# Two-layer encoder trunk on one core: weight sums of four lead pairs made earlier and kept in DRAM, x's sums in product order, fixed rings of buffers and other store queues at the end

## The chip, the cores and the metric

One NeuronCore of a Trainium2 chip runs the whole program. The metric is device time in microseconds (us) of one execution. The engines are TensorE (PE in the profile, PEld for its weight loads), VectorE (DVE), ScalarE (ACT), GpSimd (POOL) and SyncE (SP), which here only issues DMAs. Each engine works through its own queue in order.

## The reference

```python
def _sq_relu_mlp(x, w1, w2):
    return jnp.square(jax.nn.relu(x @ w1)) @ w2

def reference(x, ...):                    # x: (1, 1024, 1024), D_FF = 4096
    for i in range(2):
        y = _short_conv_mixer(x, ...) if i == 0 else _mla_mixer(x, ...)
        x = _layer_norm(ALPHA * x + y, ln_mix_g[i], ln_mix_b[i])
        x = _layer_norm(ALPHA * x + _sq_relu_mlp(x, ff_w1[i], ff_w2[i]), ln_ff_g[i], ln_ff_b[i])
    return x
```

Layer 0 mixes tokens by a gated convolution of width 3 between two projections, layer 1 by attention over latents with 8 heads. All data are float32.

## The kernel before

A float32 matrix product is made from three float32r matmuls (`mm3`, lines 108 to 112): each operand is cut into a high part, a copy on ScalarE (line 85), and a low part, a subtraction on VectorE (line 86); high x high, high x low and low x high go into one PSUM bank.

The stages follow one another: the first mixer (lines 534 to 580; `sc_channel` makes one of eight channel blocks, `piece` loads and cuts its weights, `token_out` adds a projection to a row tile of x), the MLP of layer 0, attention, the MLP of layer 1 with the output. `ffn` (line 240) is one MLP. Each of its two matrix products is done in seven products of half size instead of eight (the Strassen-Winograd scheme), so it needs sums and differences of quarter blocks of both factors.

First matrix product: the 32 row blocks of w1 form 16 pairs p. Pair p has four quarters a11, a12, a21, a22, loaded as two "act" buffers of 512 KB (`load`, line 247). `sums` (line 252) makes on GpSimd the four combinations that products 3, 5, 6 and 7 need. `operand` cuts what product k of pair p takes. `ahead` prepares six operands in advance, in the order of the list `seq`. x stands transposed: `ln_T` transposes it on TensorE, scales it on ScalarE into `st.y` and cuts it; `combine` (line 342) makes x's four combinations, for products 5, 7, 6 and 4, column block j by column block j. Products 1 and 2 need only the first half of the tokens, product 3 only the second half. So the first four pairs, the lead (`LEAD`), run products 1 and 2 first (`begin`), while the transposes of the second half go on (`st.pump`), then product 3, and then the rest (`rest`). The results are squared after the ReLU, combined, and stored in DRAM as `hs[k, p]`.

Second matrix product: for each product k in `order2` all 16 pairs accumulate in PSUM. `second` (line 381) loads a piece of h and a quarter of w2 (line 390), subtracts for the combination (line 394 for k = 4 on GpSimd, line 398 on VectorE) and cuts both. k = 4 is last: it runs over token tiles (0, 1), then 2, then 3, and loads its left operands by `left` (line 377). `done` adds a product to the output rows (line 441), and `finish` normalizes a row tile: `keep_z` in layer 0, `emit` (line 903) in layer 1, which scales, adds and stores the output. The first four row tiles are finished while k = 7 runs (`post`), the last four in the passes of k = 4.

Buffers are taken from pools: "act" (34 of 128x1024), "fp" (8, cut operands), "half" (19 of 128x512). A buffer is given out again when the last use of its tile is over. A planner in the framework orders each engine's queue and hands out the buffers ahead of time; the program text gives only priorities and dependencies.

Of the kernel before, what the change touches and what calls it, by code (L numbers as in the profile page):

```python
# [12 lines left out]
P = 128  # L13
# [25 lines left out]
def trunk_kernel(ctx, tc, x, xT, w_sci, w_sco, w_lat, w_qk, w_rv, w_o, w_f1, w_f2, gvec, grow, rope, out):  # L39
# [111 lines left out]

    def ln_stats(xr):
        s = stat(24)
# [12 lines left out]

    def ln_z(xr):
        mu, r, _ = ln_stats(xr)
        nc.vector.tensor_scalar(xr, xr, mu, r, op0=ALU.subtract, op1=ALU.mult)
# [52 lines left out]
    def last_chunk(l, lhs_of, wps, xrs, first, zs):  # L222
        st = Stage(True)
        for t in range(NT):
# [15 lines left out]
    def ffn(l, lnl, st, zs, xa, hs, out_l, finish, early=None):  # L240

# [5 lines left out]
        def load(p):  # L247
            raw[p] = [act1(F32), act1(F32)]
            for i in range(2):
                nc.sync.dma_start(raw[p][i], w_f1[l, p + NPAIR * i])  # L250

        def sums(p):
            (a11, a12), (a21, a22) = [(r[:, 0:HB], r[:, HB:T]) for r in raw[p]]
            s1 = s1w[p] = hbt()
            nc.gpsimd.tensor_tensor(s1, a21, a22, op=ALU.add)  # L255
            nc.gpsimd.tensor_tensor(a21, a11, a21, op=ALU.subtract)  # L256
            nc.gpsimd.tensor_tensor(a11, s1, a11, op=ALU.subtract)  # L257
            nc.gpsimd.tensor_tensor(a12, a12, a11, op=ALU.subtract)

        def operand(p, k):  # L260
            r1, r2 = raw[p]
            src = {1: r1[:, 0:HB], 2: r1[:, HB:T], 3: r1[:, HB:T], 4: r2[:, HB:T], 5: s1w.get(p),
                   6: r1[:, 0:HB], 7: r2[:, 0:HB]}[k]
            wh, wl = fpair()
            split(src, wh, wl)
            return wh, wl
# [6 lines left out]
        def ahead(n):  # L273
            while seq and len(ready) < n:
                p, k = seq.pop(0)
                if p not in raw:
                    load(p)
                if k == (3 if p < LEAD else 6):
                    sums(p)
                ready[p, k] = operand(p, k)  # L280
            if not seq and len(ready) < 4:
                ahead2(4 - len(ready))

        def product(p, k):
            ahead(AHEAD)
            wp = ready.pop((p, k))
            ps = psB()
# [14 lines left out]
        def rest(p):  # L302
# [36 lines left out]
            for k, a in ((1, a11), (4, a22), (5, s1), (6, s2), (7, s3), (2, a12), (3, s4)):  # L339
                nc.sync.dma_start(hs[k, p], a)  # L340

        def combine(j):
            b11, b12 = st.y[j][:, 0:HB], st.y[j][:, HB:T]
            b21, b22 = st.y[j + 4][:, 0:HB], st.y[j + 4][:, HB:T]
# [23 lines left out]
        def part(d, p):  # L368
            if p // 2 not in d:
                d[p // 2] = act1(F32)  # L370
            return d[p // 2][:, (p % 2) * HB:(p % 2 + 1) * HB]

        def left(k, p, js):
# [7 lines left out]
        def second(k, p):  # L381
# [62 lines left out]
        for k in order2[:-1]:  # L444
# [20 lines left out]
        passes = ((0, 1), (2,), (3,))  # L465
        todo = [(js, p) for js in passes for p in range(NPAIR)]
        lefts, wps = {}, {}
        for js in passes:
            pss = [psB() for _ in js]
            for p in range(NPAIR):  # L470
# [10 lines left out]
                if p % 4 == 1:  # L481
                    st2.pump(1)
                if early and js == passes[-1] and p in (10, 12, 14):
                    early()
            for j, ps in zip(js, pss):
                done(4, j, ps)
                finish(4 + j, xrs)
        if out_l is not None:
# [63 lines left out]
    for half in range(2):  # L552
# [4 lines left out]
        yt[0, half], carry = gate(0, half, *pss, carry)  # L557
    xrs = [xrt() for _ in range(NT)]
    for t in range(NT):
        nc.vector.tensor_copy(xrs[t][:, 0:1], carry[:, 0:1])  # L560
        nc.gpsimd.dma_start(xrs[t], x[t * P:(t + 1) * P])
# [12 lines left out]
    wso = [piece(w_sco[i]) for i in range(4)]  # L574
# [11 lines left out]

    def keep_z(t, xrs):
        ln_z(xrs[t])
        nc.gpsimd.dma_start(spill[t * P:(t + 1) * P], xrs[t])
# [10 lines left out]

    st, xrs = ffn(0, 0, st, zs[0], xa, hs, 1, keep_z, early_lat)
    stage.__exit__(None, None, None)
# [299 lines left out]

    def emit(t, xrs):
        if not ogr:
            ogr.extend(ln_rows(3, hbt))
        gr = ogr
        xr = xrs[t]
        mu, r, s = ln_stats(xr)
# [12 lines left out]
    ffn(1, 2, st, zs[1], xa, hs, None, emit)  # L921
    stage.__exit__(None, None, None)
# [59 lines left out]
```

## Time and profile before

| what | value |
|---|---|
| median of 3 runs | 2119.86 us (2118.95 to 2119.93) |
| profiled execution | 2118.39 us, its span 2116.6 us |
| granted TensorE clock, mean | 0.989 of full speed |
| instructions | 27650 |
| bytes moved by DMA | 299.93 MB, mean 142 GB/s |

The span runs from the first to the last instruction; the rest of the execution's own time lies around it. Busy time of an engine is the sum of its instructions' time. The view by stretches gives each engine's busy time and number of instructions (x) in a stretch, the granted clock (1.00 is 2.4 GHz, 0.50 is 1.2 GHz) and the DMA share. In a timeline, a row's last bracket says how long the engine stood idle before the instruction and whose end it waited for.

### The profile page before, as it was taken

How to read it: one execution, taken by the hardware profiler on the slowest of the kernel's cores; microseconds unless marked ns; L12 is line 12 of the kernel's file. 1: busy time of each engine (PE TensorE's matmuls, PEld its weight loads, DVE VectorE, ACT ScalarE, POOL GpSimd, SP SyncE). 2: the span in 40 equal slices, each digit the busy share in tenths (PEclk: the TensorE clock that was granted, in tenths of full speed). 3: DMA queues.
4: the chain of work that ended last, by engine and by line, in shares of the span. 5: the costliest groups of instructions: out<-in, count | busy, mean ns of one | idle time of the engine just before them, and what ended most of it. 6: DMA issues, size and time to landing. Idle time of an engine off the chain costs nothing. (4 is left out here: it accounts for less than half of the span.)

```text
span 2116.6 us, 27650 instructions
## 1 busy us (share of the span) xinstructions
PE 2051.6 (97%) x9592; PEld 1702.5 (80%) x9592; DVE 1509.2 (71%) x2586; ACT 939.9 (44%) x1775; POOL 444.9 (21%) x399
## 2 busy tenths in 40 slices
PE   8999999799999999999999999999799999999987
PEld 6888888688888788888888888778688887888865
DVE  5333438887785697878467778878986785796877
ACT  4110213554454553345556665324644464543343
POOL 1000001535651000130000002313355630000252
PEclk9999999899999999999999999999899999999998
DMA  5310213066553986643100001213256545995522
GB/s 171 120 49 31 70 53 141 31 225 212 196 197 121 362 309 200 204 131 120 50 7 22 16 27 58 88 70 130 93 197 225 207 152 195 335 339 160 183 96 77
DMA packets 151820, 299.93 MB, mean 142 GB/s; under 512 B 17008, under 2 KB 32368, under 8 KB 151680
## 3 DMA queue, kind: packets, MB, share of 16 engines
q1 hardware_dynamic: 140976, 265.88, 36.7%
q0 software_dynamic: 7392, 26.26, 3.4%
q10 hardware_dynamic: 3312, 6.03, 0.9%
q8 instruction: 75, 1.23, 0.2%
q14 instruction: 65, 0.53, 0.1%
HBM read 214.21 MB, written 83.89 MB: 141 GB/s over the span
## 5 line engine op out<-in xcount | busy, mean ns | idle before, releaser
L110 PE MATMUL pB<-act,fp 128*128 128x512 f32 x1024 | 403.4, 395 | 21.6 <-ACT act L85 14.5
L111 PE MATMUL pB<-act,fp 128*128 128x512 f32 x1024 | 402.2, 393 | 6.2 <-DVE act L86 6.2
L112 PE MATMUL pB<-act,fp 128*128 128x512 f32 x1024 | 403.2, 394 | 4.7 <-DVE fp L86 4.4
L86 DVE TENSOR_TENSOR fp<-act,fp 128x512 fp32r<-128x512 f32 x352 | 307.0, 877 | 129.1 <-ACT fp L85 128.6
L85 ACT CAST fp<-act 128x512 fp32r<-128x512 f32 x352 | 213.7, 617 | 309.3 <-PE pB L112 151.2
L111 PE MATMUL pB<-fp,act 128*128 128x512 f32 x768 | 299.4, 390 | 3.2 <-DVE fp L86 2.9
L110 PE MATMUL pB<-fp,act 128*128 128x512 f32 x768 | 297.8, 390 | 4.0 <-ACT fp L85 2.5
L112 PE MATMUL pB<-fp,act 128*128 128x512 f32 x768 | 298.6, 389 | 0.0
L110 PEld LDWEIGHTS pB<-act,fp 128*128 128x128 f32 x1024 | 193.7, 189 | 66.8 <-ACT act L85 17.4
L112 PEld LDWEIGHTS pB<-act,fp 128*128 128x128 f32 x1024 | 193.9, 189 | 51.0 <-DVE fp L86 11.2
L111 PEld LDWEIGHTS pB<-act,fp 128*128 128x128 f32 x1024 | 194.2, 190 | 47.7 <-DVE act L86 7.9
L110 PE MATMUL pB<-act,w 128*128 128x512 f32 x536 | 210.1, 393 | 6.7 <-ACT w L85 6.1
L111 PE MATMUL pB<-act,w 128*128 128x512 f32 x536 | 209.9, 392 | 0.3 <-DVE act L86 0.2
L112 PE MATMUL pB<-act,w 128*128 128x512 f32 x536 | 209.3, 391 | 0.0
L293 DVE TENSOR_TENSOR half<-half,pB 128x512 f32<-128x512 f32 x232 | 155.0, 681 | 59.7 <-PE pB L112 56.8
L110 PEld LDWEIGHTS pB<-fp,act 128*128 128x128 f32 x768 | 144.0, 188 | 35.3 <-ACT fp L85 3.4
L111 PEld LDWEIGHTS pB<-fp,act 128*128 128x128 f32 x768 | 144.2, 188 | 34.9 <-DVE fp L86 5.3
L112 PEld LDWEIGHTS pB<-fp,act 128*128 128x128 f32 x768 | 144.1, 188 | 30.0
L110 PE MATMUL pB<-w,act 128*128 128x512 f32 (+1 forms) x480 | 164.9, 344 | 1.6 <-DVE act L142 0.7
L111 PE MATMUL pB<-w,act 128*128 128x512 f32 (+1 forms) x480 | 163.4, 341 | 1.3 <-DVE w L86 1.3
L112 PE MATMUL pB<-w,act 128*128 128x512 f32 (+1 forms) x480 | 162.6, 340 | 0.0
L86 DVE TENSOR_TENSOR act<-half,act 128x512 fp32r<-128x512 f32 x198 | 147.6, 749 | 16.5 <-ACT act L85 16.3
(154 smaller groups left out, 3312.1 us busy)
## 6 DMA issues: line engine op xcount, KB each, us to landing
h<-half SPq DMA_DIRECT2D x224, 256.0 KB, 2.4
half<-h SPq DMA_DIRECT2D x192, 256.0 KB, 4.7
half<-in_w_f SPq DMA_DIRECT2D x160, 256.0 KB, 4.3
act<-in_w_f SPq DMA_DIRECT2D x64, 512.0 KB, 4.6
act<-in_w_f SPq DMA_DIRECT2D x64, 256.0 KB, 4.3
raw<-in_w_sci SPq DMA_DIRECT2D x42, 256.0 KB, 2.7
z<-act POOLq DMA_DIRECT2D x16, 512.0 KB, 3.1
act<-z SPq DMA_DIRECT2D x16, 512.0 KB, 3.9
```

The source lines that it names most:

```text
L85: nc.scalar.copy(hi, src)
L86: nc.vector.tensor_tensor(lo, src, hi.bitcast(F32), op=ALU.subtract)
L110: nc.tensor.matmul(ps, lh, rh, start=first, stop=False)
L111: nc.tensor.matmul(ps, lh, rl, start=False, stop=False)
L112: nc.tensor.matmul(ps, ll, rh, start=False, stop=last)
L293: nc.vector.tensor_tensor(o, a, b, op=op)
```

## The change

- The weight sums of the four lead pairs of both layers are made during channels 1 to 3 of the first mixer (`lead_sums`): two loads on GpSimd's queue, four GpSimd operations, three stores to DRAM tiles `ws`. A small copy from the last channel's result holds each load back to its channel. x's row tiles are loaded after that, one channel before their first use.
- In the MLP, a lead pair loads only its first row for products 1 and 2. `fetch` loads the sums of products 3 and 6 with one DMA before product 3, and those of 7 and 5, with the plain quarter of product 4, before product 6. All of them go through SyncE's queue.
- x's sums become a list of `chores`: two of the subtractions first, then the cuts for product 6, those for 7, then differences and cuts for 5 and 4. All sums of x are VectorE's. The second half's transposes come in the order 4, 0, 5, 1, 6, 2, 7, 3, four after each of the first two `begin`s.
- In k = 4, the left operands use a ring of six "half" buffers and the w2 quarters a ring of three.
- The statistics of the half of a row tile that k = 4 does not change are taken in the middle of its pass.
- The output stores leave SyncE for GpSimd's queue, except those of the last tile. Tiles 4 to 6 multiply and add on VectorE.

```diff
+    def ln_half(xr, s, d):
         st = s[:, 0:12].rearrange("p (a b) -> p a b", a=2)
-        for d in range(2):
+        nc.vector.bn_stats(st[:, d], xr[:, d * HB:(d + 1) * HB])
...
-        st.add_T(l, 1, xrs, (4, 5, 6, 7, 0, 1, 2, 3))
+        st.add_T(l, 1, xrs, (4, 0, 5, 1, 6, 2, 7, 3))
...
+    def weight_sums(r, s1):
+        (a11, a12), (a21, a22) = [(a[:, 0:HB], a[:, HB:T]) for a in r]
+        nc.gpsimd.tensor_tensor(s1, a21, a22, op=ALU.add)
+        nc.gpsimd.tensor_tensor(a21, a11, a21, op=ALU.subtract)
+        nc.gpsimd.tensor_tensor(a11, s1, a11, op=ALU.subtract)
+        nc.gpsimd.tensor_tensor(a12, a12, a11, op=ALU.subtract)
+
+    def lead_sums(l, p, ws, after):
+        r = [act1(F32), act1(F32)]
+        s1 = act1(F32)[:, 0:HB]
+        for i in range(2):
+            nc.vector.tensor_copy(r[i][:, 0:1], after)
+            nc.gpsimd.dma_start(r[i], w_f1[l, p + NPAIR * i])
+        weight_sums(r, s1)
+        nc.gpsimd.dma_start(ws[:, 0:T], r[0])
+        nc.gpsimd.dma_start(ws[:, T:T + HB], r[1][:, 0:HB])
+        nc.gpsimd.dma_start(ws[:, T + HB:2 * T], s1)
...
-            raw[p] = [act1(F32), act1(F32)]
-            for i in range(2):
-                nc.sync.dma_start(raw[p][i], w_f1[l, p + NPAIR * i])
+            raw[p] = [act1(F32) for _ in range(1 if p < LEAD else 2)]
+            for i, r in enumerate(raw[p]):
+                nc.sync.dma_start(r, w_f1[l, p + NPAIR * i])
...
+        def fetch(p, k):
+            if k == 3:
+                raw[p] = [act1(F32), None]
+                nc.sync.dma_start(raw[p][0], ws[p][:, 0:T])
+            else:
+                raw[p][1] = act1(F32)
+                nc.sync.dma_start(raw[p][1][:, 0:HB], ws[p][:, T:T + HB])
+                nc.sync.dma_start(raw[p][1][:, HB:T], w_f1[l, p + NPAIR, :, HB:T])
+                s1w[p] = hbt()
+                nc.sync.dma_start(s1w[p], ws[p][:, T + HB:2 * T])
...
-                if k == (3 if p < LEAD else 6):
+                if p < LEAD and k in (3, 6):
+                    fetch(p, k)
+                elif k == 6:
                     sums(p)
...
+        def chore(k):
+            while len(xc.get(k, ())) < 4:
+                chores.pop(0)()
+
         def product(p, k):
             ahead(AHEAD)
+            chore(k)
...
         def combine(j):
-            for k, o, a, b in ((5, b11, b12, b11), (7, b12, b22, b12), (6, b22, b22, b11), (4, b21, b22, b21)):
-                (nc.gpsimd if k == 7 else nc.vector).tensor_tensor(o, a, b, op=ALU.subtract)
-                h, lo = act()
-                split(o, h, lo)
-                xc.setdefault(k, []).append((h, lo))
+            add(block(12, j), block(22, j), block(12, j), ALU.subtract)
+            add(block(11, j), block(12, j), block(11, j))
+
+        def diff(k, b, j):
+            a = (22, 11) if k == 5 else (11, 21)
+            add(block(b, j), block(a[0], j), block(a[1], j), ALU.subtract)
+            cut(k, b, j)
+
+        chores += [lambda j=j: combine(j) for j in range(4)]
+        chores += [lambda j=j: cut(6, 11, j) for j in range(4)] + [lambda j=j: cut(7, 12, j) for j in range(4)]
+        chores += [lambda j=j: diff(5, 22, j) for j in range(4)] + [lambda j=j: diff(4, 21, j) for j in range(4)]
...
-        for p in range(LEAD):
+        for p, n in enumerate((4, 4, 0, 0)):
             begin(p)
-            st.pump(2)
+            st.pump(n)
+            if p:
+                for _ in range(2 if p < 3 else 4):
+                    chores.pop(0)()
...
             add(held[p][2], held[p][0], product(p, 3))
-            combine(p)
+            for _ in range(2):
+                chores.pop(0)()
...
+            if not lring:
+                lring.extend(hbt() for _ in range(6))
...
-            hr = hbt()[:, 0:n]
+            hr = lring[nleft[0] % len(lring)][:, 0:n]
+            nleft[0] += 1
...
-            w = part(ta, p) if k == 1 else part(tb, p) if k == 3 else hbt()
+            if k == 4 and not wring:
+                wring.extend(hbt() for _ in range(3))
+            w = part(ta, p) if k == 1 else part(tb, p) if k == 3 else wring[p % 3] if k == 4 else hbt()
...
+                if p == 9:
+                    for j in js:
+                        half_stats(j)
...
-    for c in range(1, 5):
-        sc_channel(c)
+    for c in range(1, 4):
+        for l, p in early_sums[3 * c - 3:3 * c]:
+            lead_sums(l, p, wss[l][p], carry[:, 0:1])
+        carry = sc_channel(c)
+    xrs = [xrt() for _ in range(NT)]
+    for t in range(NT):
+        nc.vector.tensor_copy(xrs[t][:, 0:1], carry[:, 0:1])
+        nc.gpsimd.dma_start(xrs[t], x[t * P:(t + 1) * P])
+    sc_channel(4)
...
-            if t == NT - 1 or (t == NT - 2 and d == 0):
+            if t == NT - 1:
...
-                (nc.gpsimd if d else nc.vector).tensor_tensor(xr[:, c], xr[:, c], gr[d], op=ALU.mult)
-                nc.gpsimd.tensor_tensor(xr[:, c], xr[:, c], gr[2 + d], op=ALU.add)
-            (nc.scalar if t == NT - 1 and d == 0 else nc.sync).dma_start(out[t * P:(t + 1) * P, c], xr[:, c])
+                last = t >= NT // 2
+                (nc.gpsimd if d and not last else nc.vector).tensor_tensor(xr[:, c], xr[:, c], gr[d], op=ALU.mult)
+                (nc.vector if last else nc.gpsimd).tensor_tensor(xr[:, c], xr[:, c], gr[2 + d], op=ALU.add)
+            (nc.sync if t == NT - 1 and d else nc.scalar if t == NT - 1 else nc.gpsimd).dma_start(
+                out[t * P:(t + 1) * P, c], xr[:, c])
```

## Rows read from the trace of the kernel before

**Rows 1.** The page, share of busy time: us, share, instructions.

```profile
PE 2051.6 (97%) x9592; PEld 1702.5 (80%) x9592; DVE 1509.2 (71%) x2586; ACT 939.9 (44%) x1775; POOL 444.9 (21%) x399
```

**Rows 2.** View by stretches: stretch, length, busy us (x instructions), clock, DMA share, GB/s.

```profile
47.00:176.00 129.00, 129.00 (x571) 106.85 (x570) 50.23 (x94) 25.32 (x45) 4.22 (x8) 1.00 0.25 87
176.00:361.00 185.00, 185.00 (x834) 153.73 (x833) 86.71 (x162) 33.18 (x59) 3.20 (x6) 1.00 0.22 74
390.00:421.00 31.00, 20.14 (x73) 14.56 (x71) 28.43 (x40) 17.78 (x32) 9.65 (x7) 0.78 0.05 17
1485.00:1515.00 30.00, 18.85 (x67) 13.72 (x66) 27.43 (x39) 16.48 (x30) 9.39 (x7) 0.77 0.05 18
2005.00:2048.00 43.00, 40.09 (x175) 32.17 (x174) 43.00 (x65) 20.82 (x39) 29.01 (x18) 1.00 0.33 108
2048.00:2084.00 36.00, 29.04 (x107) 21.04 (x106) 15.73 (x38) 9.15 (x25) 5.09 (x4) 0.86 0.24 72
2084.00:2107.60 23.60, 22.89 (x98) 17.71 (x96) 22.09 (x56) 10.74 (x33) 11.05 (x8) 1.00 0.25 87
2107.60:2116.60 9.00, 0.26 (x2) 0.00 (x0) 5.15 (x12) 0.29 (x1) 0.12 (x1) 0.65 0.23 87
```

**Rows 3.** Timeline of the first lead: start, length, engine, line, operation, idle before.

```profile
362.86 0.50 PE L110 MATMUL pB<-act,fp 128*128 128x512 f32 x1 [0.71 <-ACT fp L85]
...
372.82 33.59 SPq L340 DMA_DIRECT2D h<-half  x4
...
381.17 1.04 PE L174 MATMUL pB<-ident,act 128*128 128x128 f32 x8
...
382.10 0.62 ACT L85 CAST fp<-act 128x512 fp32r<-128x512 f32 x1 [3.34 <-POOL act L258]
...
389.48 3.48 DVE L346 TENSOR_TENSOR act<-act 128x512 f32<-128x512 f32 x2
...
401.90 0.68 DVE L86 TENSOR_TENSOR fp<-half,fp 128x512 fp32r<-128x512 f32 x1
402.50 0.68 DVE L346 TENSOR_TENSOR act<-act 128x512 f32<-128x512 f32 x1
...
413.62 1.22 PE L110 MATMUL pB<-act,fp 128*128 128x512 f32 x2 [6.15 <-ACT act L85]
```

**Rows 4.** Groups of GpSimd's instructions: count, busy us, mean ns, idle before.

```profile
L255 POOL TENSOR_TENSOR half<-act 128x512 f32<-128x512 f32 x32 | 44.8, 1401 | 36.1 <-ACT half L329 36.1
...
L918 POOL TENSOR_TENSOR act<-act,half 128x512 f32<-128x512 f32 x13 | 20.7, 1610 | 1.5 <-DVE act L917 1.2
...
L227 POOL DMA_DIRECT2D z<-act x16 | 8.6, 536 | 373.1 <-DVE act L169 333.8 <-DVE stat L163 25.4 <-PE pB L112 13.9
```

**Rows 5.** Timeline of the second layer's tail.

```profile
2040.31 1.74 POOL L394 TENSOR_TENSOR act<-act,half 128x512 f32<-128x512 f32 x1
...
2048.38 0.34 SPq L390 DMA_DIRECT2D half<-in_w_f  x1
...
2050.45 0.39 PE L110 MATMUL pB<-act,fp 128*128 128x512 f32 x1
...
2051.50 1.29 POOL L394 TENSOR_TENSOR act<-act,half 128x512 f32<-128x512 f32 x1 [9.46 <-DMA half<-in_w_f]
...
2052.83 0.62 ACT L85 CAST act<-act 128x512 fp32r<-128x512 f32 x1 [8.99 <-POOL act L394]
```

**Rows 6.** Waits of SyncE's queue, 2030 to 2066: total us, times, longest.

```profile
SPq L919 <- POOL act L918: 8.5, 4, 3.4
SPq L390 <- DVE fp L86: 6.2, 1, 6.2
```

**Rows 7.** The page, DMA issues: count, KB each, median us to landing.

```profile
act<-in_w_f SPq DMA_DIRECT2D x64, 512.0 KB, 4.6
```

**Rows 8.** Timeline of the end, the ScalarE queue's store.

```profile
2112.63 0.35 ACTq L919 DMA_DIRECT2D out<-act  x1
```

More of the change, by code (lines that the diff above doesn't have):

```diff
@@ L150, in newton, with ln_stats @@
         nc.vector.tensor_tensor(r, r, t, op=ALU.mult)
-    def ln_stats(xr):
-        s = stat(24)
+    def ln_half(xr, s, d):
         st = s[:, 0:12].rearrange("p (a b) -> p a b", a=2)
-        for d in range(2):
+        nc.vector.bn_stats(st[:, d], xr[:, d * HB:(d + 1) * HB])
+    def ln_stats(xr, s=None):
+        cols = (0, 1) if s is None else (0,)
+        s = stat(24) if s is None else s
+        st = s[:, 0:12].rearrange("p (a b) -> p a b", a=2)
+        for d in cols:
             nc.vector.bn_stats(st[:, d], xr[:, d * HB:(d + 1) * HB])
@@ L165, in ln_stats, with ln_z @@
         return mv[:, 0:1], r, s
-    def ln_z(xr):
-        mu, r, _ = ln_stats(xr)
+    def ln_z(xr, s=None):
+        mu, r, _ = ln_stats(xr, s)
         nc.vector.tensor_scalar(xr, xr, mu, r, op0=ALU.subtract, op1=ALU.mult)
@@ L236, in trunk_kernel, with ffn @@
     LEAD = 4
+    def weight_sums(r, s1):
[14 more added lines that the diff above has]
+        nc.gpsimd.dma_start(ws[:, T + HB:2 * T], s1)
     AHEAD = 6
     AHEAD2 = 4
-    def ffn(l, lnl, st, zs, xa, hs, out_l, finish, early=None):
+    def ffn(l, lnl, st, zs, xa, hs, ws, out_l, finish, early=None):
         xc = {1: st.xt[0][0:4], 2: st.xt[0][4:8]}
@@ L247, in load @@
         def load(p):
-            raw[p] = [act1(F32), act1(F32)]
-            for i in range(2):
-                nc.sync.dma_start(raw[p][i], w_f1[l, p + NPAIR * i])
+            raw[p] = [act1(F32) for _ in range(1 if p < LEAD else 2)]
+            for i, r in enumerate(raw[p]):
+                nc.sync.dma_start(r, w_f1[l, p + NPAIR * i])
         def sums(p):
[L253 to L258, printed above, removed]
+            s1w[p] = hbt()
+            weight_sums(raw[p], s1w[p])
+        def fetch(p, k):
[6 more added lines that the diff above has]
+                nc.sync.dma_start(raw[p][1][:, HB:T], w_f1[l, p + NPAIR, :, HB:T])
+                s1w[p] = hbt()
+                nc.sync.dma_start(s1w[p], ws[p][:, T + HB:2 * T])
         def operand(p, k):
-            r1, r2 = raw[p]
-            src = {1: r1[:, 0:HB], 2: r1[:, HB:T], 3: r1[:, HB:T], 4: r2[:, HB:T], 5: s1w.get(p),
-                   6: r1[:, 0:HB], 7: r2[:, 0:HB]}[k]
+            src = s1w[p] if k == 5 else raw[p][k in (4, 7)]
+            if k != 5:
+                src = src[:, 0:HB] if k in (1, 6, 7) else src[:, HB:T]
             wh, wl = fpair()
@@ L340, in rest, with block, cut @@
                 nc.sync.dma_start(hs[k, p], a)
+        def block(k, j):
+            return {11: st.y[j][:, 0:HB], 12: st.y[j][:, HB:T],
+                    21: st.y[j + 4][:, 0:HB], 22: st.y[j + 4][:, HB:T]}[k]
         def combine(j):
-            b11, b12 = st.y[j][:, 0:HB], st.y[j][:, HB:T]
-            b21, b22 = st.y[j + 4][:, 0:HB], st.y[j + 4][:, HB:T]
-            for k, o, a, b in ((5, b11, b12, b11), (7, b12, b22, b12), (6, b22, b22, b11), (4, b21, b22, b21)):
-                (nc.gpsimd if k == 7 else nc.vector).tensor_tensor(o, a, b, op=ALU.subtract)
-                h, lo = act()
-                split(o, h, lo)
-                xc.setdefault(k, []).append((h, lo))
+            add(block(12, j), block(22, j), block(12, j), ALU.subtract)
+            add(block(11, j), block(12, j), block(11, j))
+        def cut(k, b, j):
+            h, lo = act()
+            split(block(b, j), h, lo)
+            xc.setdefault(k, []).append((h, lo))
+        def diff(k, b, j):
[5 more added lines that the diff above has]
+        chores += [lambda j=j: diff(5, 22, j) for j in range(4)] + [lambda j=j: diff(4, 21, j) for j in range(4)]
         for p in range(LEAD):
             load(p)
-        for p in range(LEAD):
+        for p, n in enumerate((4, 4, 0, 0)):
             begin(p)
-            st.pump(2)
+            st.pump(n)
+            if p:
+                for _ in range(2 if p < 3 else 4):
+                    chores.pop(0)()
         st.pump(len(st.todo))
@@ L465, in ffn, with half_stats @@
         passes = ((0, 1), (2,), (3,))
+        early_s = {}
+        def half_stats(j):
+            early_s[j] = stat(24)
+            ln_half(xrs[4 + j], early_s[j], 1)
         todo = [(js, p) for js in passes for p in range(NPAIR)]
@@ L486, in ffn @@
                 done(4, j, ps)
-                finish(4 + j, xrs)
+                finish(4 + j, xrs, early_s[j])
         if out_l is not None:
@@ L557, in trunk_kernel @@
         yt[0, half], carry = gate(0, half, *pss, carry)
[L558 to L561, printed above, removed]
     def sc_channel(c):
@@ L570, in sc_channel @@
             yt[c, half], carry = gate(c, half, *pss, carry)
-    for c in range(1, 5):
-        sc_channel(c)
+        return carry
+    wss = [[dr.tile([P, 2 * T], F32, name="ws%d_%d" % (l, p)) for p in range(LEAD)] for l in range(DEPTH)]
+    early_sums = [(l, p) for l in range(DEPTH) for p in range(LEAD)]
+    for c in range(1, 4):
[7 more added lines that the diff above has]
+    sc_channel(4)
     wso = [piece(w_sco[i]) for i in range(4)]
@@ L585, in trunk_kernel, with keep_z @@
     spill = dr.tile([T, D], F32, name="spill")
-    def keep_z(t, xrs):
-        ln_z(xrs[t])
+    def keep_z(t, xrs, s=None):
+        ln_z(xrs[t], s)
         nc.gpsimd.dma_start(spill[t * P:(t + 1) * P], xrs[t])
@@ L901, in trunk_kernel, with emit @@
     ogr = []
-    def emit(t, xrs):
+    def emit(t, xrs, s=None):
         if not ogr:
@@ L907, in emit @@
         xr = xrs[t]
-        mu, r, s = ln_stats(xr)
+        mu, r, s = ln_stats(xr, s)
         nc.vector.tensor_scalar(s[:, 17:18], mu, r, -1.0, op0=ALU.mult, op1=ALU.mult)
```

6 lines of the change are left out of this document (4 added, 2 removed).

## The prediction

> **What bounds the kernel now.** I read the share of busy time first: TensorE is busy 97% of the span [rows 1], so the time is TensorE's work plus its holes, and this change takes no matmul away. Only a hole that is filled can shorten it, so I looked for holes next, with the view that cuts the span into stretches [rows 2]. The full pace is in the row 176 to 361: 834 matmuls in 185.00 us, 0.222 us each. Held against that pace, four stretches of [rows 2] are short of matmuls:
>
> - first lead, 390 to 421: 73 matmuls are worth 16.2 us, the stretch has 31.0, so 14.8 are lost;
> - second lead, 1485 to 1515: 67 are worth 14.9 of 30.0, 15.1 lost;
> - tail, 2005 to 2107.6: 38.8 of 43.0, 23.7 of 36.0 and 21.7 of 23.6, so 4.2, 12.3 and 1.9 lost, 18.4 together;
> - the end, 9.0 us in which TensorE has nothing left.
>
> The granted clock is part of this: it is 1.00 at full pace (2.4 GHz) and 0.78, 0.77 and 0.86 in the three worst stretches, that is, some of their matmuls ran at 1.2 GHz, after TensorE had stood still. A count held against the full pace holds the waits and the clock together, so neither is added again. Outside these four, the start apart, the holes are small, and the change does not touch them.
>
> The timeline says why the leads are short [rows 3]. GpSimd makes the four weight sums of four lead pairs just when VectorE wants to make x's sums. ScalarE stood 3.34 us before a weight cast, until a GpSimd sum (L258) came, and VectorE's subtractions queue behind such casts. When VectorE gets to x's sums, two of them take 3.48 us beside GpSimd (389.48), 1.74 each, against 0.68 when GpSimd is still (402.50). Then combine runs j by j over all four products, so the four pieces of the first product needed (k = 6) come last to first hand: TensorE waits 6.15 us in one place (413.62), for a cast of x.
>
> In the tail the timeline shows another chain [rows 5, 6]. SyncE's queue is in order. It stands at output stores (L919) until GpSimd's additions are through, 8.5 us in four waits, then 6.2 us at a load of w2 (2048.38), whose "half" buffer had last served a piece of h whose split on VectorE was late. The GpSimd subtraction behind that load starts after 9.46 us of idleness (2051.50), ScalarE's cast of it at 2052.83, and behind that cast, in the same queue, stands the cast of a left operand that TensorE waits for. The same goes on at the next three pairs; most of the 12.3 us lies in these four gaps.
>
> **The change part by part.** *Lead sums made early.* Per layer it takes 16 GpSimd operations out of the lead and puts 32 in all into the first mixer, at 1.40 us each by the row of L255 [rows 4]: 45 us of GpSimd between 47 and 176, where GpSimd is busy 4.22 of 129 us [rows 2]. If each slows one VectorE instruction from 0.68 to 1.74 us [rows 3], VectorE gets 32 x 1.06 = 34 us on top of 50.23, 84 of 129 us. TensorE runs that stretch at full pace (571 in 129.00), so the cover is 45 us of VectorE idleness; without it, at most those 34 us would be paid. Lower bound 0, upper bound 34; I take 0. The Trainium skill ("SBUF — State Buffer", Who interferes with whom) says that a VectorE instruction with two SBUF inputs and a GpSimd instruction that reads SBUF exclude one another, the later one waiting out the other. The 1.74 beside 0.68 us [rows 3] agrees, and the rule speaks against the new place of the sums as much as for emptying the old one; by it, too, the first mixer pays 34 us of VectorE time, which idleness covers.
>
> The loads and stores of the sums ride on GpSimd's own queue, 5 DMAs a pair, 40 in all at 0.54 us of issue (L227, [rows 4]), 22 us. Sums and issue make 67 of 129 us. x's eight loads now stand behind them on that queue and start a channel (144 x 0.222 = 32 us) before their first use; a load of 512 KB lands in 4.6 us [rows 7]. I cost that at nothing; if the queue is late by more than that channel, the residual additions wait, and I give that up to 10 us in the range only.
>
> *The lead after it.* The fetches are SyncE's: per pair one half-megabyte load instead of two, then one of 512 KB and three of 256 KB. SyncE stood 33.59 us at four stores here [rows 3], so it has the room, if the fetches come ahead of those stores. No GpSimd arithmetic is left in the lead, so VectorE's price is 0.60 us from start to start (401.90 to 402.50, [rows 3]). Up to the product k = 4 of pair 0 it has 21 weight cuts, 4 cuts of x^T, 16 x sums, 16 cuts of these and 13 additions of products, 70 instructions, 42 us, and some 3 us of the last LayerNorm (estimate): from 362 to 407. TensorE, from 362.86, needs 15 products x 12 x 0.222 = 40.0 us and four double groups of transposes at 0.8 us net (1.04 us shown for one, [rows 3]), 3.2 us: it wants the last product at 406 and the last x piece at 408. So the order by product just fits, and VectorE is the tight engine. A queue never runs without gaps; I leave 3 us of loss in each lead. Lower bound 0, upper 8: the "act" buffers. By my count, x^T (12), y (8) and the three finished products' x pieces (12) hold 32 of 34 when k = 4 wants its first, and weights of pairs 2 and 3 want the other two; a wait like the 6.15 us at 413.62 can come back there. Gain 14.8 - 3 + 15.1 - 3 = 23.9 us.
>
> *Rings and stores.* The w2 loads of k = 4 get three buffers of their own, the left pieces six. Load p then waits for subtraction p - 3 and no longer for a VectorE split. Stores on GpSimd's queue no longer stop SyncE. They come behind the additions they wait for on the same engine, so they block nothing new but GpSimd itself: eight stores x 0.54 = 4.3 us in the stretch 2005 to 2048, where it is busy 29.01 of 43 [rows 2]. The last subtractions then start near 2040.31 + 4.3 = 2045 [rows 5]; five of them, two with a load of about 2.5 us ahead, are through by 2053, and TensorE, whose k = 4 begins at 2050.45 [rows 5] and takes six matmuls, 1.33 us, a pair, wants the first of these five at 2050.5 + 11 x 1.33 = 2065. The wait goes; of the 12.3 us I leave 2. VectorE is busy 43.00 of 43.00 us just before [rows 2] and is not relieved, so the 4.2 stay, and the 1.9 stay: tiles 4 to 6 give VectorE ten more operations, 6.0 us at 0.60, less two longer ones of today, and take GpSimd's, 1.61 us each [rows 4], from beside its splits. Gain 10.3; bounds 0 (the same wait at another buffer) and 15.
>
> The Trainium skill ("SBUF — State Buffer", Summary: rules for kernel authors) advises against a GpSimd-queue DMA under VectorE work, because descriptor writing is starved while VectorE is in a two-port mode; its section A bandwidth-pool intuition that's wrong gives about 3.1 us for one so overlapped. The stores of z took 0.54 us on GpSimd beside a working VectorE [rows 4], so the trace does not show it here; by the page, eight stores would be 25 us instead of 4.3.
>
> *The rest.* The statistics of one half ahead of time: TensorE does not wait for them, and in the chain after the last matmul one such instruction stands now too; 0. After the last matmul the chain to the ScalarE store at 2112.63 and its landing [rows 8] is the same: 9.0 us stay. Rings in the first layer: no hole there, 0.
>
> **Sum.** 23.9 + 10.3 = 34.2 us off the profiled execution's 2118.39 gives 2084.2; the median of the runs is 1.5 above it, so 2085.7, forecast 2086.
>
> **The rivals.** *The tail keeps its wait*: GpSimd's queue is late (eight stores at several times 0.54 us, or subtractions ordered behind all of them), or a late left split stops SyncE before the w2 load as it does now. For it: VectorE at 43.00 of 43.00; against: ring buffers free long before. Then 23.9 only: 2096. *The act buffers bind in the leads*: each keeps 8 us: 2096. For it: my count of 34; against: each finished x sum frees two buffers. *Both*: 2106. *Fetches late*, the other side: a fetch gets its act buffer only when an earlier pair's last cut frees one, or stands in SyncE's queue behind a store that waits for ScalarE, as L340 does for 33.59 us [rows 3]. Each that TensorE sees costs 4.6 us of load [rows 7] and 1.3 of cast and subtraction, 5.9 us; there are eight groups a layer, 16. Six of them eat the 34.2; ten give 2145. Against it: these loads depend on nothing but a buffer, and can go out while the last LayerNorm runs. *The change does not do what it says*: VectorE, with the same 32 x operations, is the bound of the lead anyway and the rest goes on as it is: only some 3 us a lead and the tail's, 2104. Against it: its 28.43 busy us in 390 to 421 [rows 2] come after idling earlier, behind GpSimd.
>
> **Chances.** Forecast 0.53 (its own range 2079 to 2093: 1 to 5 us left in each lead, 7 to 13 gained in the tail), tail keeps its wait 0.15, act buffers 0.12, both 0.05, no relief 0.05, late fetches 0.07, cancelling within 0.2% (4 us, about what a measurement tells from no change) 0.03. Range 2075 (nothing left in the leads, 15 gained in the tail) to 2106: it holds the forecast and all rivals but late fetches. Faster 0.90, same 0.03, slower 0.07.
>
> **What would show it.** Right: in both leads some 135 to 140 matmuls per 31 us and clock 1.00, no GpSimd sums there, x sums at 0.6 us; no SyncE wait at a w2 load of k = 4 over 2 us, no 9 us GpSimd gap; the first mixer still at 0.222 us a matmul. Wrong: a TensorE wait for a cast of x at k = 5 or 4 of pair 0; waits of SyncE's fetches for a buffer; left splits late behind VectorE in the last passes, or GpSimd sums still running when x's loads should go out.

## The result, and the profile after

The changed kernel takes 2083.36 us in the median (2080.19 to 2086.86) against 2119.89: ratio 0.9831, 95% interval 0.9818 to 0.9843, or 35.8 us less (33.3 to 38.6). The forecast was 2086, its range 2075 to 2106. The profiled execution is the longest of the four, 2086.86 us with a span of 2085.1. Line numbers are those of the changed kernel: L456 is the GpSimd subtraction for k = 4 (L394 before), L437 and L452 SyncE's loads of h and w2 (L377, L390), L332 VectorE's additions (L346, L293), L994 to L996 the multiplication, addition and store of the last LayerNorm (L917 to L919). Cuts are still L85 and L86.

The page's row of busy shares answers to [rows 1]: TensorE's instructions are the same 9592.

```profile
PE 2044.7 (98%) x9592; PEld 1706.3 (82%) x9592; DVE 1505.8 (72%) x2618; ACT 938.8 (45%) x1776; POOL 453.0 (22%) x437
```

The view by stretches, with the columns of [rows 2]. The first mixer and the stretch after it come first, then the two leads, then the tail cut in the same lengths as there, counted back from the end of the span:

```profile
47.00:176.00 129.00, 129.00 (x571) 106.92 (x570) 71.65 (x109) 25.13 (x45) 67.28 (x80) 1.00 0.66 218
176.00:361.00 185.00, 185.00 (x835) 153.79 (x834) 86.76 (x162) 33.61 (x60) 3.20 (x6) 1.00 0.20 66
390.00:421.00 31.00, 31.00 (x139) 25.67 (x138) 28.33 (x47) 19.05 (x35) 0.28 (x1) 1.00 0.60 201
1470.00:1500.00 30.00, 30.00 (x134) 24.88 (x133) 27.98 (x47) 19.20 (x35) 0.00 (x0) 1.00 0.60 198
1973.50:2016.50 43.00, 40.76 (x173) 33.24 (x173) 43.00 (x63) 21.32 (x41) 39.65 (x28) 0.96 0.34 109
2016.50:2052.50 36.00, 31.19 (x128) 25.29 (x127) 20.41 (x45) 10.56 (x28) 9.24 (x5) 0.91 0.24 73
2052.50:2076.10 23.60, 22.92 (x100) 18.04 (x98) 18.90 (x62) 11.01 (x34) 3.24 (x6) 1.00 0.37 118
2076.10:2085.10 9.00, 0.36 (x2) 0.00 (x0) 5.15 (x12) 0.29 (x1) 0.00 (x0) 0.81 0.19 73
```

At 0.222 us a matmul the leads lose nothing: 139 matmuls are worth 30.9 of 31.0 us, 134 are worth 29.7 of 30.0, at the full clock (2.4 GHz). The whole 14.8 + 15.1 us is back. The tail's three stretches held 380 matmuls before and hold 401 now, worth 89.0 of 102.6 us: 13.6 us are still lost where 18.2 were (the prediction's 18.4, with its rounding). So the tail gave 4.6 us. The end is 9.0 us as before.

The timeline of the first lead answers to [rows 3]. VectorE makes x's sums early and at 0.6 us each. SyncE's fetches of product 3's sums (L282) are out by 378.0, and the fetches before product 6 (L285) begin right behind them; their last ones go out between 393 and 399:

```profile
372.09 0.69 DVE L332 TENSOR_TENSOR act<-act 128x512 f32<-128x512 f32 x1 [1.36 <-ACT act L180]
...
375.16 1.89 DVE L332 TENSOR_TENSOR act<-act 128x512 f32<-128x512 f32 x3
...
376.69 1.29 SPq L282 DMA_DIRECT2D act<-ws  x3
...
378.08 0.38 SPq L285 DMA_DIRECT2D act<-ws  x1
...
382.50 1.89 DVE L332 TENSOR_TENSOR act<-act 128x512 f32<-128x512 f32 x3
```

TensorE's list of waits from 361 to 421 has one row left, where [rows 3] had a single wait of 6.15 us:

```profile
PE pB L110 <- ACT fp L85: 0.7, 1, 0.7
```

GpSimd's groups answer to [rows 4]: one of the four sums, as it runs in the first mixer, and the stores of the last LayerNorm from 1960 to 2052.

```profile
L246 POOL TENSOR_TENSOR act<-act 128x512 f32<-128x512 f32 x8 | 10.4, 1297 | 0.3
...
L996 POOL DMA_DIRECT2D out<-act x8 | 4.5, 564 | 0.3 <-POOL act L995 0.3
```

The tail's timeline answers to [rows 5, 6]. It has a new chain:

```profile
2009.64 1.52 ACT L992 ACTIVATE act<-act,stat 128x512 f32<-128x512 f32 x2 [6.80 <-DVE stat L985]
...
2011.25 10.94 POOL L994 TENSOR_TENSOR act<-act,half 128x512 f32<-128x512 f32 x1 [2.16 <-ACT act L992]
2011.33 0.68 DVE L994 TENSOR_TENSOR act<-act,half 128x512 f32<-128x512 f32 x1
2011.93 1.28 DVE L86 TENSOR_TENSOR act<-act 128x512 fp32r<-128x512 f32 x2
...
2019.15 1.88 DVE L86 TENSOR_TENSOR act<-act 128x512 fp32r<-128x512 f32 x3
2022.15 2.52 POOL L995 TENSOR_TENSOR act<-act,half 128x512 f32<-128x512 f32 x2
2024.62 1.11 POOL L996 DMA_DIRECT2D out<-act  x2
2027.92 0.62 ACT L85 CAST act<-act 128x512 fp32r<-128x512 f32 x1 [9.48 <-DMA out<-act]
2028.45 1.93 ACT L85 CAST fp<-half 128x256 fp32r<-128x256 f32 x6
...
2028.90 0.80 PE L110 MATMUL pB<-act,fp 128*128 128x512 f32 x1 [4.81 <-ACT fp L85]
```

Read it from the bottom. TensorE waits 4.81 us for a left operand's cast. That cast stands on ScalarE behind the cast of a w2 piece, which has waited 9.48 us for an "act" buffer. The buffer is that of output tile 3, whose store came at 2024.62, after two additions, after a multiplication (L994) that took 10.94 us where its kind takes 1.3 to 1.75. It started while VectorE was in one subtraction, and VectorE went on with sixteen more instructions that have both inputs in SBUF, without a pause; the last ended at 2021.03.

The wait that the rings were to take away is gone. The last L456 ends at 1991.87, when the first tile's L994 begins; before, five came after 2040. In SyncE's waits from 1973.5 to 2076.1 none at the load of w2 is over 1.3 us ([rows 6] had 6.2 in one); its long ones are at loads into the left ring, and none of TensorE's waits leads back to them:

```profile
SPq L437 <- DVE fp L86: 69.7, 26, 41.9
SPq L452 <- POOL act L456: 8.9, 9, 1.3
```

Of the page's DMA issues [rows 7], the early loads on GpSimd's queue land a little later; the last row is the store that answers to [rows 8], 3.87 us before the end of the span (3.97 before):

```profile
act<-in_w_f POOLq DMA_DIRECT2D x16, 512.0 KB, 5.1
```

```profile
2081.23 0.35 ACTq L996 DMA_DIRECT2D out<-act  x1
```

### The profile page after: what moved, and what is told of

The parts are those of the page before. It is cut to its first block, busy times and chain, and to the rows that moved or that the text cites. A ratio compares the mean times of both kernels' runs of the same rounds, so it can differ in the third digit from the quotient of the medians.

```text
span 2085.1 us, 27812 instructions
## 1 busy us (share of the span) xinstructions
PE 2044.7 (98%) x9592; PEld 1706.3 (82%) x9592; DVE 1505.8 (72%) x2618; ACT 938.8 (45%) x1776; POOL 453.0 (22%) x437
## 4 chain that ended last, share of the span: by engine, by line
PE 84%; DVE 6%; DMA 3%; POOL 2%; ACT 2%; issue 2%; SPq 0%; DVEq 0%; ACTq 0%; POOLq 0%
PE pB L112 26%; PE pB L111 26%; PE pB L110 26%; DVE act L86 1%; PE pB L881 1%; DVE fp L86 1%; PE pB L179 1%; DMA raw<-in_w_o 1%; DMA half<-in_w_f 1%; DMA act<-in_xT 1%; ACT tmp L752 1%; PE pA L849 1%; POOL act L994 1%; PE pA L850 1%; PE pA L851 1%
## 5 line engine op out<-in xcount | busy, mean ns | idle before, releaser
L86 DVE TENSOR_TENSOR fp<-act,fp 128x512 fp32r<-128x512 f32 x352 | 294.8, 843 | 117.3 <-ACT fp L85 116.8
L85 ACT CAST fp<-act 128x512 fp32r<-128x512 f32 x352 | 212.9, 617 | 274.9 <-PE pB L112 139.2
L332 DVE TENSOR_TENSOR half<-half,pB 128x512 f32<-128x512 f32 x232 | 155.2, 681 | 67.2 <-PE pB L112 64.3
L86 DVE TENSOR_TENSOR act<-half,act 128x512 fp32r<-128x512 f32 x198 | 151.2, 769 | 15.4 <-ACT act L85 15.4
```

The costliest lines, as they stand in the source:

```text
L85: nc.scalar.copy(hi, src)
L86: nc.vector.tensor_tensor(lo, src, hi.bitcast(F32), op=ALU.subtract)
L332: nc.vector.tensor_tensor(o, a, b, op=op)
```

## Experiments

"Gain" is (1 - ratio) x 2119.9 us, with the ratio's interval. "Tail lost" is 102.6 us less 0.222 us for each matmul in the three tail stretches of the run's profile, cut as above. The changed kernel: gain 35.8, tail lost 13.6; the kernel before: 0 and 18.2.

| run | median us | ratio (95%) | gain us | tail lost us |
|---|---|---|---|---|
| lead_only | 2088.45 | 0.9865 (0.9850 to 0.9879) | 28.6 | 19.1 |
| tail_only | 2114.21 | 0.9985 (0.9975 to 0.9995) | 3.2 | 8.7 |
| dram_only | 2097.00 | 0.9905 (0.9891 to 0.9920) | 20.1 | |
| order_only | 2114.78 | 0.9985 (0.9976 to 0.9994) | 3.2 | |
| dve_emit | 2074.13 | 0.9782 (0.9768 to 0.9797) | 46.2 | 2.9 |
| rings_only | 2084.29 | 0.9834 (0.9815 to 0.9853) | 35.2 | 11.1 |
| no_rings | 2091.75 | 0.9867 (0.9851 to 0.9884) | 28.2 | 18.5 |
| sp_stores | 2082.68 | 0.9821 (0.9805 to 0.9837) | 37.9 | 11.8 |
| tile3_dve | 2077.25 | 0.9800 (0.9787 to 0.9814) | 42.4 | 5.6 |
| dve_norings | 2080.57 | 0.9818 (0.9804 to 0.9831) | 38.6 | 10.2 |
| dve_nohalf | 2071.93 | 0.9775 (0.9762 to 0.9788) | 47.7 | 0.9 |
| dve_sp | 2075.28 | 0.9795 (0.9782 to 0.9808) | 43.5 | 3.4 |

### The lead and the tail apart

lead_only takes the tail's edits back; tail_only keeps only them, on the kernel before.

```diff
 # lead_only, against the changed kernel
-            hr = lring[nleft[0] % len(lring)][:, 0:n]
+            hr = hbt()[:, 0:n]
-            w = ... else wring[p % 3] if k == 4 else hbt()
+            w = ... else hbt()
-                if p == 9:
-                    for j in js:
-                        half_stats(j)
 # and the last LayerNorm with its stores as before
```

> The changed kernel's lead (sums of four pairs kept in DRAM, x's sums by product) with the tail of the kernel before. Theory, from the trace after the change: the leads run at full pace, so all of their loss goes, 14.8 + 15.1 = 30 us: about 2090, and the tail's stretch loses its 18 us as before. Rival, the prediction as written: the leads keep 3 us each and the tail gave 10: about 2096.

> The lead of the kernel before with the rings, early half statistics, new last LayerNorm and GpSimd stores. Theory: the tail's gain is only about 5 us (13.5 lost after against 18.4 before): about 2115. Rival, the prediction as written: 10.3 us, about 2109.5.

lead_only gained 28.6 us (25.7 to 31.8). That holds the 30 that the traces give and not the 23.9 of the prediction; its 2088.45 is near the theory's 2090. tail_only gained 3.2 (1.1 to 5.3): less than the 10.3 of the prediction. The two make 31.8, the whole change 35.8; the intervals leave that difference open. tail_only's own profile leaves it open too: it shows 8.7 us lost in the tail, a gain of 9.5, in an execution of 2111.44 us; that is one of the shortest of its nine, which go up to 2116.86. The multiplication that takes 10.94 us in the changed kernel takes 1.31 there (see "The held multiplication").

### The lead's two parts

dram_only has the sums in DRAM and x's sums in the old order, with one of the four x sums (k = 7) on GpSimd again and the second half's transposes in their old order. order_only has the four pairs' weight sums on GpSimd in the lead, and x's sums by product, all on VectorE. Both have the old tail. "The order" below means these edits together: product order, the k = 7 sums moved to VectorE, the transposes' order. No run takes them apart.

```diff
 # dram_only, against lead_only
-            chore(k)
-        for p, n in enumerate((4, 4, 0, 0)):
+        for p in range(LEAD):
             begin(p)
-            st.pump(n)
+            st.pump(2)
-            for _ in range(2):
-                chores.pop(0)()
+            combine(p)
```

> Weight sums kept in DRAM, but x's sums in the old order (tile by tile over all four products, k = 7 on GpSimd), old tail. Theory: both parts are needed. GpSimd's 16 sums are gone from the lead, but the first product still gets its pieces last, and the 6 us wait of each lead stays: 30 - 12 = 18 us gained, about 2102. Rival A, contention with GpSimd is all: about 2090, no wait for x's casts. Rival B, the order is all: under 5 us gained, 2115 or more.

> x's sums by product and all on VectorE, but the four pairs' weight sums made in the lead by GpSimd as before; old tail. Theory: both parts are needed. The weight sums still hold up weight casts and double the price of VectorE's sums: about 12 us gained, 2108, with VectorE's subtractions at some 1.7 us beside GpSimd. Rival A, contention is all: 2115 or more. Rival B, the order is all: about 2090.

dram_only came out at 20.1 (17.0 to 23.1), as the theory had it. order_only gained 3.2 (1.3 to 5.1), not 12: here the rival "contention is all" comes closer. Counted from 361 to 421, the first lead holds 213 matmuls before, 223 with the order alone, 260 with the DRAM sums alone and 278 with both. VectorE's groups from 375 to 421 in order_only say why the order is worth little by itself:

```profile
L300 DVE TENSOR_TENSOR act<-act 128x512 f32<-128x512 f32 x15 | 20.5, 1407 | 0.0
```

Fifteen x sums at 1407 ns, beside GpSimd sums of 1620. VectorE is full for the whole stretch, so another order alone can't bring the pieces in time:

```profile
390.00:421.00 31.00, 23.38 (x90) 17.52 (x89) 31.00 (x45) 17.74 (x33) 5.80 (x4) 0.94 0.07 26
```

In the changed kernel, from 361 to 421, the same instruction costs half:

```profile
L332 DVE TENSOR_TENSOR act<-act 128x512 f32<-128x512 f32 x16 | 10.4, 686 | 1.4 <-ACT act L180 1.4
```

With GpSimd's weight sums out of the way the order is worth the rest: 28.6 - 20.1 = 8.5 us, with about 3 us of uncertainty on either figure. The wait that it takes away is smaller in dram_only than the 6 us of before, so the theory had the gain right and the wait too long. In the second lead TensorE stands at

```profile
1488.00 1.22 PE L110 MATMUL pB<-act,fp 128*128 128x512 f32 x2 [2.46 <-ACT act L85]
```

The two parts do not seem additive, 20.1 + 3.2 against 28.6; the difference is about what the intervals allow. The first lead's counts go the same way: 47 and 10 matmuls more by one part alone, 65 by both. That fits an order that pays once VectorE has the time for it.

### The held multiplication

dve_emit takes GpSimd's arithmetic out of the last LayerNorm; sp_stores leaves it there and changes only the queue of the stores.

```diff
 # dve_emit, against the changed kernel
-                last = t >= NT // 2
+                last = True
 # tile3_dve, instead
+                last = t >= 3
```

> The changed kernel with the last LayerNorm's multiplications and additions of tiles 0 to 3 on VectorE too (GpSimd keeps only the stores there). Theory: one GpSimd operation held for 10.94 us at 2011.25 by VectorE's run of subtractions started the tail's rest: addition, store, the output tile's act buffer, ScalarE's cast waiting 9.48 us and six casts behind it. Without it ScalarE's wait and TensorE's 4.81 us go; VectorE pays 12 more operations x 0.6 = 7 us, spread: 3 to 5 us faster than the changed kernel. Rival, VectorE's load alone bounds the tail: its 7 us more come on top, 3 to 7 us slower than the changed kernel.

> The changed kernel with the output stores of tiles 0 to 6 issued by SyncE again. Theory: with GpSimd's addition late by 10 us, SyncE stands at its store and the loads of w2 and h behind it stand too: 3 to 6 us slower. Rival, the loads are far enough ahead: same within 1 us. Rival, GpSimd's issue of the stores is itself a price: 1 to 4 us faster.

dve_emit is 10.4 us better than the changed kernel (46.2 against 35.8), more than the theory's 3 to 5. The rival, VectorE's load as the bound, falls: VectorE got twelve more operations in a stretch where it had been busy without a gap, and TensorE now runs at full pace. The first two tail stretches of dve_emit:

```profile
1960.70:2003.70 43.00, 43.00 (x191) 35.63 (x190) 41.60 (x70) 23.32 (x44) 28.15 (x22) 1.00 0.50 162
2003.70:2039.70 36.00, 36.00 (x160) 29.81 (x159) 29.52 (x61) 14.49 (x35) 1.08 (x2) 1.00 0.23 74
```

The 10.4 us hold more than the one operation of the theory. In the first of these stretches the changed kernel has 173 matmuls against 191 here, 4.0 us: there VectorE and GpSimd's LayerNorm take turns, single VectorE subtractions take up to 3.10 us (at 2001.64), and TensorE waits 2.24 us for one of them (at 2008.81). In the second, where TensorE feels the held operation, it has 128 against 160, 7.1 us.

sp_stores gained 37.9, within the intervals of the changed kernel: with this split of the work the stores' queue makes no difference, neither as the theory had it (3 to 6 us slower) nor through GpSimd's issue. SyncE stands at stores for up to 14.8 us at a time there, and the rival that had the loads far enough ahead holds. Its GpSimd timeline has the same operation with the same length:

```profile
2006.32 10.95 POOL L994 TENSOR_TENSOR act<-act,half 128x512 f32<-128x512 f32 x1 [3.03 <-ACT act L992]
```

and VectorE's unbroken run there ends at 14.23 + 1.88 = 2016.11:

```profile
2014.23 1.88 DVE L86 TENSOR_TENSOR act<-act 128x512 fp32r<-128x512 f32 x3
```

In both kernels the operation ends 1.16 us after the run (2022.19 - 2021.03, 2017.27 - 2016.11).

Such a run of VectorE does not by itself hold the operation up. tail_only has the same tail code, and VectorE is as dense there (43.00 of 43.00 us). Tile 3's multiplication (L939 there) starts 0.53 us into a VectorE subtraction, 0.52 in the changed kernel, and VectorE's instructions before and behind it are the same ones in the same order. Yet it takes 1.31 us, and VectorE's next instruction is the one that waits, 1.78 us:

```profile
2040.38 1.31 POOL L939 TENSOR_TENSOR act<-act,half 128x512 f32<-128x512 f32 x1 [1.44 <-ACT act L937]
...
2039.85 0.68 DVE L86 TENSOR_TENSOR fp<-act,fp 128x512 fp32r<-128x512 f32 x1
2040.45 1.78 DVE L939 TENSOR_TENSOR act<-act,half 128x512 f32<-128x512 f32 x1
```

The kernel before (1.69 us), lead_only (1.33), rings_only (1.67) and no_rings (1.38) do not hold it either. So the hold is shown where it stands, but what decides between a hold and taking turns is not. Every kernel has one profile, so it is not shown either whether its other executions had the same hold.

> The changed kernel with tile 3's three GpSimd operations of the last LayerNorm alone on VectorE; those of tiles 0 to 2 stay on GpSimd. Theory, one held operation: the multiplication that took 10.94 us was tile 3's, so this alone takes back most of the 9 us that moving all twelve took back: 2074 to 2078. Rival, it is the number of GpSimd operations beside VectorE's run: a quarter of them is worth a quarter, some 2 us, 2081; or the hold moves to tile 2's: 2083.

One tile's three operations moved give 42.4 us, 6.6 of the 10.4 that all twelve give: a quarter of the operations, nearly two thirds of the effect, and no GpSimd operation of the LayerNorm above 1.75 us. The time, 2077.25, is what the theory said, so in the changed kernel the one held operation is the larger part. The 3.8 us to dve_emit lie at the edge of the intervals (2077.25, 2074.97 to 2079.62, against 2074.13); tile3_dve's profile has 5.6 us lost in the tail against 2.9.

### The rings

> The changed kernel without the rings: left pieces and w2 loads draw on the shared half buffers. Theory: the wait of SyncE at a w2 load for a VectorE split comes back, 2 to 4 us slower. Rival, stores off SyncE are the gain and the rings do nothing: same within 1 us.

> The changed kernel with the old last LayerNorm (GpSimd additions up to tile 6, stores on SyncE) and without early half statistics: of the tail only the rings stay. Theory: the rings free the load behind which TensorE waited, but SyncE stands at stores again; 2 to 4 us slower than the changed kernel. Rival, the rings are the tail's whole gain: same within 1 us. Rival, GpSimd's stores and the new split of the work are its whole gain: 5 us slower, as without any of the tail.

> All multiplications and additions of the last LayerNorm on VectorE, without the rings. Theory: two waits in a row. The w2 load of k = 4 stands behind a VectorE split of a left piece whatever GpSimd does, so the four 2 us waits of TensorE for weight casts are back: 2088 to 2092. Rival, GpSimd's share of the LayerNorm was the whole cause and the rings are only a cover for it: 2074 to 2077.

no_rings puts the shared "half" buffers back in the changed kernel (`hbt()` for `lring` and `wring`, as in the diff above); rings_only keeps the rings but has the old last LayerNorm; dve_norings is no_rings with `last = True`. Without the rings the change's tail is worth nothing that shows: 28.2 against 28.6 for the lead alone. With the rings and the old LayerNorm all of it is there, 35.2 against 35.8. So the new split of the LayerNorm, GpSimd's stores and the early statistics together gave no measurable time, and my 2 to 4 us for either run were wrong: no_rings costs 7.6 against the changed kernel, rings_only 0.6.

The equal time of rings_only and the changed kernel is made of different losses, though. In the three tail stretches the changed kernel loses 4.6, 7.6 and 1.4 us, rings_only 3.3, 2.5 and 5.4, by one profile each (the four executions of rings_only go from 2080.35 to 2089.30, and the profile is of the shortest). rings_only has no held operation. But in its last pass SyncE stands at the output stores (L992) as the theory said, the next load of h goes out at 2054.97 behind them, and ScalarE waits 4.75 us for it:

```profile
2046.00:2069.60 23.60, 21.25 (x82) 15.48 (x80) 18.71 (x45) 9.26 (x27) 10.78 (x8) 0.93 0.36 120
...
2051.13 3.75 SPq L992 DMA_DIRECT2D out<-act  x3
...
2056.93 0.30 ACT L85 CAST fp<-half 128x128 fp32r<-128x128 f32 x1 [4.75 <-DMA half<-h]
```

By these profiles the changed kernel is spared most of that loss and pays for the hold instead. In sp_stores, with the stores on SyncE but tiles 4 to 6 on VectorE, the last stretch loses 2.5 us.

GpSimd's timeline in no_rings shows the old gap before the fourth-last L451 (the L456 there), as in [rows 5]:

```profile
2025.91 1.28 POOL L451 TENSOR_TENSOR act<-act,half 128x512 f32<-128x512 f32 x1 [9.33 <-DMA half<-in_w_f]
```

The four corners, gain in us:

| | GpSimd arithmetic for tiles 0 to 3 | none |
|---|---|---|
| shared buffers | 28.2 | 38.6 |
| rings | 35.8 | 46.2 |

Rings are worth 7.6 us in both columns, and taking GpSimd's arithmetic out 10.4 in both rows. That the figures agree to the tenth is partly chance, as each has an interval of about 3 us either way. My theory of dve_norings, two waits in a row of which either keeps all the loss, gave 2088 to 2092; it took 2080.57, so it falls: the two edits add up, within the intervals. The 10.4 of the upper row can't be the held multiplication, since no_rings has none. There the gain lies mostly in the first tail stretch, where VectorE and GpSimd take turns: 165 matmuls in no_rings, 192 in dve_norings, 6.0 us. In dve_norings a subtraction is held in the same way, behind a VectorE run that ends at 6.68 + 1.28 = 2007.96:

```profile
2004.27 4.84 POOL L451 TENSOR_TENSOR act<-act,half 128x512 f32<-128x512 f32 x1
...
2006.68 1.28 DVE L86 TENSOR_TENSOR act<-act 128x512 fp32r<-128x512 f32 x2
```

It ends 1.15 us behind that run.

### What is left of the tail's edits

> All multiplications and additions of the last LayerNorm on VectorE, without the statistics of one half ahead of time (both layers). Theory, as in the prediction: they hide nothing that TensorE waits for, same within 1 us of 2074. Rival: the chain after the last matmul gets one more instruction of some 0.6 us, and each earlier tile's LayerNorm is later: 1 to 3 us slower.

> All multiplications and additions of the last LayerNorm on VectorE and the output stores of tiles 0 to 6 on SyncE. Theory: SyncE stands at a store only until VectorE's addition, which is not late, and the rings hold loads enough: same within 1.5 us of 2074. Rival: loads of h and w2 behind those stores come late for the left pieces, 3 to 6 us slower.

dve_nohalf (dve_emit without `half_stats`) gained 47.7 (44.9 to 50.5), dve_sp (dve_emit with the stores on SyncE) 43.5 (40.7 to 46.2); both hold dve_emit's 46.2 in their intervals, dve_sp at the upper end. Early statistics and the stores' queue are worth nothing that shows here, once VectorE has all of the last LayerNorm's multiplications and additions. dve_nohalf has the shortest time of all, 2071.93 us: ratio 0.9775 to the kernel before, and below the changed kernel by 11 us. In its tail TensorE loses 0.9 us; what remains is the end, 9.0 us.

## Why the prediction came out right, point by point

The total was right, 2086 against 2083.36, but by the traces two terms were off by about 6 us each, in opposite directions, so its closeness is luck.

- **The holes.** The four losses at 0.222 us a matmul were the right list: the leads' part came back whole, and with dve_nohalf all of the tail's but 0.9 us.
- **The first mixer at nothing.** Right. 571 matmuls in 129.00 us as before. GpSimd is busy 67.28 us (67 worked out). VectorE pays 71.65 - 50.23 = 21.4 us, inside the bounds 0 to 34, and its idleness covers it. x's loads behind the sums cost nothing: 835 matmuls in the next 185 us.
- **The leads, 23.9 us.** Mechanism right, size off: the 3 us that I left in each measured 0. It was a margin for gaps in VectorE's queue, taken from no row; [rows 2] has VectorE at 43.00 of 43.00 us without one. lead_only's 28.6 (25.7 to 31.8) and 139 and 134 matmuls stand in its place. "Act buffers bind", "no relief" and "late fetches" did not happen: TensorE waits 0.7 us in the whole lead.
- **The price of GpSimd beside VectorE** was the step that carried the leads, and it is now shown: 1407 against 686 ns for the same sum, and 20.1 us for taking the weight sums away alone.
- **The tail, 10.3 us.** This failed at "The wait goes; of the 12.3 us I leave 2". The sentence before it, that the stores "block nothing new but GpSimd itself", did not fail: sp_stores puts them back on SyncE and finds the same time and the same hold. The old wait went as written, even earlier than written: the subtractions were through by 1991.87 (the end of the last L456), not shortly before TensorE needs them. But I costed GpSimd's last LayerNorm at its usual 1.3 to 1.75 us a row and never asked who waits for its buffers. One of these operations, tile 3's, took 10.94 us beside an unbroken run of VectorE. The chain from there to TensorE was an "act" buffer, the resource that I had counted for the leads only. The loss of that stretch went from 12.3 to 36.0 - 128 x 0.222 = 7.6 us. The rival "the tail keeps its wait" had the right place and the wrong cause (a late store queue or a late split). In tail_only, whose profile has no hold, the tail loses 8.7 us, a gain of 9.5, near the 10.3; its nine executions, though, gained only 3.2.
- **The 4.2 and the 1.9 us**, said to stay, stay in the changed kernel: 43.0 - 173 x 0.222 = 4.6 and 23.6 - 100 x 0.222 = 1.4. But the reason for the first, that VectorE at 43.00 of 43.00 is not relieved, is wrong: in dve_emit, with more to do, VectorE is busy 41.60 us there with 70 instructions instead of 43.00 with 63, and TensorE loses 0.6. VectorE's busy time held waits for GpSimd, such as the 3.10 us of one subtraction.
- **The stores at 0.54 us** were right: 0.564 in the mean. The Trainium skill ("SBUF — State Buffer", A bandwidth-pool intuition that's wrong) has about 3.1 us for a DMA of GpSimd's queue that overlaps a VectorE `tensor_copy`; no store here shows that, and sp_stores finds no difference. The Trainium skill's other rule (the same page, Who interferes with whom, and Summary: rules for kernel authors), that the later of two such instructions waits until the first is finished, agrees in kind with the held operations. It does not give their length: L994 came in one subtraction and waited out sixteen instructions more, while in tail_only it waited out none.
- **The end and the early statistics**: 9.0 us and nothing, as written.

What stays open: the profiled execution's span is 31.5 us shorter, and leads and tail give 29.9 + 4.6 = 34.5. The 3 us of difference lie in the stretches between: from the second lead to the tail TensorE loses 13.8 us before (2145 matmuls in 490.0 us, from 1515) and 15.5 after (2063 in 473.5, from 1500), which is more than half of it. The cause is open, and the four executions spread over 6.7 us. Open too is what decides whether a GpSimd operation takes turns with VectorE or is held through its run. The small statistics instructions between VectorE's, near tiles 0 to 2, don't explain it alone, as in tail_only the same instructions surround tile 3's multiplication as in the changed kernel and it isn't held; no run tested it.

## What to carry to other kernels

When a wait is taken away, cost the next chain too: what runs beside each of its operations, and who waits for their buffers. A GpSimd operation with SBUF inputs beside a VectorE without pauses cost time in either way seen here: the two took turns and VectorE paid, or GpSimd was held. So keep GpSimd's arithmetic off any chain whose output buffer the next stage needs; moving it to an engine that shows 100% busy can still be a gain. When two variants take the same time, look whether they lose it in the same place. Price a reordering only after the contention in its stretch is gone: here the same order of x's sums was worth 3 us with GpSimd's weight sums beside it and 8.5 without.

## What was not expected of the hardware

A GpSimd 128x512 operation that usually took 1.3 to 1.75 us took 10.94, 10.95 and 4.84 us beside an unbroken run of VectorE instructions with both inputs in SBUF. It ended 1.16, 1.16 and 1.15 us after the run, as if it had done almost nothing before. VectorE's own instructions ran at their usual 0.6 us from start to start meanwhile. In tail_only the same operation at the same place took 1.31 us, and VectorE's next instruction 1.78. Where the two engines took turns, as at the sums of the leads, VectorE paid 1407 ns in the mean instead of 686, and GpSimd 1620.
